# Up-projection units of a convolutional feed-forward: fewer pairs with a unit, another order inside

## The chip, the cores and the metric

The kernel runs on one core of one Trainium2 chip. The metric is the device time of one execution in microseconds, as the median of several runs; lower is better. Every input and weight is float32 and lies in the chip's memory.

## What is computed

A trunk of two layers over 256 positions of width 2048: mixer A (grouped-query attention), a feed-forward, mixer B (dilated windows), a second feed-forward, and a last normalisation. The change lies in the two feed-forwards:

```python
def conv_ffn(h, w_up, conv_w, conv_b, w_down):
    u = h @ w_up                       # 2048 -> 2 * 5632
    u = depthwise_conv(u, conv_w) + conv_b    # width 3 over positions
    gate, val = jnp.split(u, 2, axis=-1)
    return (jax.nn.silu(gate) * val) @ w_down

h = h + conv_ffn(rms_norm(h, ffn_norm[i]), w_up[i], conv_w[i], conv_b[i], w_down[i])
```

## The kernel before

**Products.** Every float32 weight tile of 128 x 1024 is loaded (`raw`), rounded by ScalarE into a high part (`wh`, L144 or L180), and VectorE subtracts that to get the low part (`wl`, L145 or L181). The activations have such pairs too. A product is three matmuls: high by high, high by low, low by high. There are four buffers each for `raw`, `wh` and `wl`, and within a feed-forward every third `raw` comes from a further pool.

**Pairs.** The up-projection has 22 blocks of 512 columns: 11 for the gate, 11 for the value. Block p of the gate and block p of the value make a pair; in the code the first pair is p = 0. The pairs 0 to 5 are the first half, 6 to 10 the second; behind each half its part of the down-projection runs. The depth 2048 is cut into four groups `kg` of 512. A plain `feed` does one group of one block: 48 matmuls for both blocks, 24 each, which need two splits per block.

**Units.** In `fast_unit` one group of both blocks is done with seven block products instead of eight: 42 matmuls. It splits seven weight tiles, of which four are sums of others, formed in place by VectorE ahead of their split (L179): the dictionary `sums` says which, and the loop takes the products in the order 1, 2, 3, 5, 7, 6, 4. Before the change each such sum is told to issue only after the previous split (`tc.issue_after`). The unit's products go into four more accumulators (`ps`), which the lines L695 to L704 of `up_pair` recombine. `UP` names the pairs with a unit; `UP_ORDER` puts it fourth in the pair, behind three plain feeds of the gate and ahead of three of the value. The down-projections and mixer B's output projection have units too, with spots of their own for the sums (`spot`); those always had a free order of sums.

**Work beside the matmuls.** What follows a block (evacuation with the scale, transposition into `u` with VectorE and 16 GpSimd copies, the convolution on ScalarE and VectorE, the silu, the product, splitting the result) is written as generators: `gate_gen`, `value_gen`, `flush`. `start` runs one to its first `yield` and puts it into the list `pending`, which is worked off first in, first out. `step()` moves the first of `pending` on by one `yield`; `step(True)` moves all in the list `beside`. A plain feed calls `step` once per 128 rows of depth, in turn for the one and for the other list; a unit calls it after each of its seven products. The order of calls, with a priority for splits that places them 60 instructions ahead, decides in which order each engine has its instructions; each engine works in that order. `sums` (started ahead of the first feed of the half) prepares the activation's own sums for the units, in slots with the numbers 20 or 16; `bias_lines` prepares mixer B's bias in three slots.

## Time and profile before

| | us |
|---|---|
| median of 3 runs | 2245.68 |
| fastest, slowest | 2245.32, 2246.84 |
| the profiled execution's own time | 2248.19 |
| its span, first to last instruction | 2246.4 |
| PE, DVE, ACT, POOL busy | 2220.4, 1902.1, 1350.8, 745.0 |

The span is what the traced instructions cover; the execution's own time also has what lies around them. PE is TensorE, PEld its weight loads, DVE VectorE, ACT ScalarE, POOL GpSimd, SP the engine that issues most loads. Busy time is the union of the shown durations; a matmul's shown duration overlaps the next one's, so a busy PE can still lose time between the starts of its matmuls. A row of a list of groups has line, engine, operation, output <- inputs, shapes and count, then busy time and mean duration in ns, then the idle time before and who ended it.

### The profile page before, as it was taken

What the parts mean: (1) busy time and instruction counts of PE and PEld (TensorE: products, weight loads), DVE (VectorE), ACT (ScalarE), POOL (GpSimd) and SP (SyncE); (2) the same over time, 40 slices, a digit from 0 to 9 for tenths busy, and PEclk for the clock granted to TensorE, in tenths of its full rate; (3) what the DMA queues carried; (4) which work ended last, traced back from release to release, by engine and by line L of the source; (5) the groups of instructions that cost most, each with busy time, mean ns of one, the idle gap of its engine ahead of it and who ended that gap; (6) DMA issues with size and microseconds to landing.
All of it is one profiled execution on the core that took longest, in us unless ns stands there. A gap on an engine that the chain in (4) does not pass through costs nothing.

```text
span 2246.4 us, 28935 instructions
## 1 busy us (share of the span) xinstructions
PE 2220.4 (99%) x9945; PEld 1830.8 (81%) x9945; DVE 1902.1 (85%) x2415; ACT 1350.8 (60%) x1902; POOL 745.0 (33%) x1017
## 2 busy tenths in 40 slices
PE   9999999999999999999999999999999999999998
PEld 7888888888887788888888888888887878877887
DVE  6877678998899997968886878687899998999887
ACT  7666656666455566665454456566666755556664
POOL 2333254652004662030053006003645600255511
PEclk9999999999999999999999999999999999999999
DMA  8665665565656566666656555656566565646664
GB/s 304 192 213 175 221 193 184 194 197 194 205 182 208 178 205 197 197 188 199 189 185 196 180 187 186 193 186 213 169 204 198 196 197 193 204 160 207 224 196 142
DMA packets 126181, 439.60 MB, mean 196 GB/s; under 512 B 14408, under 2 KB 18248, under 8 KB 126032
## 3 DMA queue, kind: packets, MB, share of 16 engines
q1 hardware_dynamic: 123056, 429.05, 58.7%
q0 software_dynamic: 2688, 8.39, 1.5%
q8 instruction: 78, 1.28, 0.2%
q14 instruction: 71, 0.58, 0.1%
q10 hardware_dynamic: 288, 0.30, 0.0%
HBM read 432.34 MB, written 5.34 MB: 195 GB/s over the span
## 4 chain that ended last, share of the span: by engine, by line
PE 43%; DVE 9%; issue 2%; DMA 1%; ACT 1%; POOL 1%; DVEq 0%; POOLq 0%; ACTq 0%
PE acc L133 13%; PE acc L132 13%; PE acc L134 13%; DVE wl L145 3%; DVE wl L181 2%; DVE raw L179 1%; DMA raw<-in_w_b_dram 1%; PE ps L188 1%; PE ps L189 1%; PE ps L187 1%; DVE cv L549 1%; DMA raw<-in_w_down_dram 0%; DVE tT L386 0%; PE acc L188 0%; PE acc L187 0%
## 5 line engine op out<-in xcount | busy, mean ns | idle before, releaser
L145 DVE TENSOR_TENSOR wl<-raw,wh 128x1024 fp32r<-128x1024 f32 (+1 forms) x708 | 882.6, 1258 | 199.6 <-ACT wh L144 194.5
L144 ACT ACTIVATE wh<-raw 128x1024 fp32r<-128x1024 f32 (+1 forms) x708 | 737.1, 1048 | 517.5 <-PE acc L134 404.1
L133 PE MATMUL acc<-wl,xh 128*128 128x512 f32 x2016 | 787.5, 391 | 2.7 <-DVE wl L145 2.5
L132 PE MATMUL acc<-wh,xh 128*128 128x512 f32 x2016 | 786.2, 391 | 0.0
L134 PE MATMUL acc<-wh,xh 128*128 128x512 f32 x2016 | 785.3, 390 | 0.0
L562 POOL COPY u<-quad 32x256 f32<-32x256 f32 x672 | 503.1, 749 | 463.3 <-DVE quad L377 426.2
L133 PEld LDWEIGHTS acc<-wl,xh 128*128 128x128 f32 x2016 | 379.1, 188 | 85.7 <-DVE wl L145 9.2
L134 PEld LDWEIGHTS acc<-wh,xh 128*128 128x128 f32 x2016 | 378.8, 188 | 78.7
L132 PEld LDWEIGHTS acc<-wh,xh 128*128 128x128 f32 x2016 | 379.2, 188 | 77.8
L132 PE MATMUL acc<-wh,a 128*128 128x512 f32 x720 | 280.9, 390 | 0.0
L133 PE MATMUL acc<-wl,a 128*128 128x512 f32 x720 | 280.4, 389 | 0.0
L134 PE MATMUL acc<-wh,a 128*128 128x512 f32 x720 | 280.0, 389 | 0.0
L180 ACT ACTIVATE wh<-raw 128x1024 fp32r<-128x1024 f32 x126 | 133.3, 1059 | 121.6 <-PE acc L134 72.2
L181 DVE TENSOR_TENSOR wl<-raw,wh 128x1024 fp32r<-128x1024 f32 x126 | 156.9, 1248 | 8.5 <-ACT wh L180 7.9
L134 PEld LDWEIGHTS acc<-wh,a 128*128 128x128 f32 x720 | 135.1, 188 | 28.3 <-DVE a L328 0.2
L133 PEld LDWEIGHTS acc<-wl,a 128*128 128x128 f32 x720 | 135.2, 188 | 28.0 <-DVE wl L145 0.5
L132 PEld LDWEIGHTS acc<-wh,a 128*128 128x128 f32 x720 | 135.2, 188 | 27.5
L381 POOL COPY wide<-quad 32x256 f32<-32x256 f32 x133 | 89.7, 674 | 168.2 <-DVE quad L377 159.8
L398 POOL COPY wide<-quad 32x256 f32<-32x256 f32 x88 | 53.1, 603 | 241.9 <-DVE quad L377 174.8
L489 ACT ACTIVATE stg<-acc,rstd 128x512 f32<-128x512 f32 x122 | 81.3, 681 | 28.8 <-PE acc L134 15.9
L549 DVE SCALAR_TENSOR_TENSOR cg<-u,cw,cg 128x256 f32<-128x256 f32 x176 | 92.7, 570 | 3.3 <-ACT cg L541 3.2
L549 DVE SCALAR_TENSOR_TENSOR cv<-u,cw,cv 128x256 f32<-128x256 f32 x176 | 90.0, 565 | 0.2
(309 smaller groups left out, 2267.6 us busy)
## 6 DMA issues: line engine op xcount, KB each, us to landing
raw<-in_w_up_dram SPq DMA_DIRECT2D x352, 512.0 KB, 4.5
raw<-in_w_down_dram SPq DMA_DIRECT2D x176, 512.0 KB, 4.6
raw<-in_w_b_dram SPq DMA_DIRECT2D x144, 512.0 KB, 4.4
raw<-in_w_bo_dram SPq DMA_DIRECT2D x48, 512.0 KB, 4.3
raw<-in_w_a_dram SPq DMA_DIRECT2D x40, 512.0 KB, 4.8
raw<-in_w_ao_dram SPq DMA_DIRECT2D x32, 512.0 KB, 4.6
raw<-in_w_a_dram SPq DMA_DIRECT2D x16, 256.0 KB, 6.0
there<-quad POOLq DMA_DIRECT2D x6, 512.0 KB, 3.8
```

Source lines behind the costliest of these rows:

```text
L132: nc.tensor.matmul(accs[m], xh, wh[:, j, :], start=st, stop=False)
L133: nc.tensor.matmul(accs[m], xh, wl[:, j, :], start=False, stop=False)
L134: nc.tensor.matmul(accs[m], xl, wh[:, j, :], start=False, stop=sp)
L144: nc.scalar.activation(wh[:, c], r[:, c], AF.Copy)
L145: newest[0] = nc.vector.tensor_tensor(wl[:, c], r[:, c], wh[:, c].bitcast(F32), ALU.subtract)
L180: nc.scalar.activation(wh, r, AF.Copy)
L181: done = nc.vector.tensor_tensor(wl, r, wh.bitcast(F32), ALU.subtract)
L381: nc.gpsimd.tensor_copy(o[32 * c:32 * c + 32, :, 32 * q:32 * q + 32], quad[32 * q:32 * q + 32, c])
L398: nc.gpsimd.tensor_copy(dst, src)
L489: nc.scalar.activation(o[:, m, :], accs[m], AF.Copy, scale=rstd[:, m:m + 1])
L549: nc.vector.scalar_tensor_tensor(cj, halves(flat[:, j, o:o + NT])[:, ::-1], tap(n, j, i), cj, ALU.mult, ALU.add)
L562: nc.gpsimd.tensor_copy(o, src)
```

## The change

`UP` loses the pair p = 7, so the third, fifth, seventh and ninth pair (p = 2, 4, 6, 8) have a unit, and the eighth is done with plain feeds. The sums of a unit are no longer told to follow the previous split. In an up-projection unit (`spot is None`) the loop no longer calls `step`. The gate's generator of a pair with a unit is put into `beside` instead of `pending`, and takes three more yields ahead of the last pair's product. The slots of `sums` are 16 in both halves, and `bias_lines` uses the slots 22, 20 and 14 for 14, 16 and 18.

```diff
-UP = 2, 4, 6, 7, 8
+UP = 2, 4, 6, 8
...
                 if q in sums:
-                    with tc.issue_after(done.ins) if spot is None else ExitStack():
-                        nc.vector.tensor_tensor(*sums[q], ALU.add)
+                    nc.vector.tensor_tensor(*sums[q], ALU.add)
                 nc.scalar.activation(wh, r, AF.Copy)
-                done = nc.vector.tensor_tensor(wl, r, wh.bitcast(F32), ALU.subtract)
+                nc.vector.tensor_tensor(wl, r, wh.bitcast(F32), ALU.subtract)
...
             begun.add(q)
-            step(i % 2 == 0)
+            if spot is not None:
+                step(i % 2 == 0)
...
                 if value is not None:
-                    for _ in range(2 if blk[0] == 1 else 1):
+                    for _ in range(4 if blk[0] in UP else 2 if blk[0] == 1 else 1):
                         yield
...
                     def gate_done(accs, gate=gate, last_value=last_value):
-                        start(gate_gen(accs, gate, last_value))
-
-                    first = partial(sums, 0, (20, 16)[hf], cg, cv)
+                        gen = gate_gen(accs, gate, last_value)
+                        if gate[0] in UP:
+                            next(gen)
+                            beside.append(gen)
+                        else:
+                            start(gen)
+
+                    first = partial(sums, 0, 16, cg, cv)
...
-        oc, oh, ln = (pair_slot(kt, [P, 1024], dt, t) for kt, t, dt in ((14, "oc", F32), (16, "oh", F32R), (18, "ln", F32)))
+        oc, oh, ln = (pair_slot(kt, [P, 1024], dt, t) for kt, t, dt in ((22, "oc", F32), (20, "oh", F32R), (14, "ln", F32)))
```

Around the unit a line of the change has a number lower by one: its sums are L178, its splits' two halves L179 and L180, its matmuls L186 to L188.

VectorE's order in the unit of the fifth pair in the first feed-forward, before. L181 is a split, L179 a sum of weights; L321 splits the activation of the third pair.

```order
L145 TENSOR_TENSOR wl_4286<-raw_4263,wh_4285 128x1024
L181 TENSOR_TENSOR wl_4315<-raw_4306,wh_4314 128x1024
L181 TENSOR_TENSOR wl_4325<-raw_4308,wh_4324 128x1024
L179 TENSOR_TENSOR raw_4306<-raw_4306,raw_4312 128x1024
L321 TENSOR_TENSOR s_4340<-st_4334,s_4339 128x1024
L181 TENSOR_TENSOR wl_4349<-raw_4310,wh_4348 128x1024
L179 TENSOR_TENSOR raw_4312<-raw_4312,raw_4310 128x1024
L181 TENSOR_TENSOR wl_4360<-raw_4306,wh_4359 128x1024
L179 TENSOR_TENSOR raw_4310<-raw_4306,raw_4310 128x1024
L181 TENSOR_TENSOR wl_4371<-raw_4312,wh_4370 128x1024
L179 TENSOR_TENSOR raw_4308<-raw_4310,raw_4308 128x1024
L181 TENSOR_TENSOR wl_4382<-raw_4310,wh_4381 128x1024
```

The same place in the change, where L180 is the split and L178 the sum:

```order
L145 TENSOR_TENSOR wl_4286<-raw_4263,wh_4285 128x1024
L180 TENSOR_TENSOR wl_4315<-raw_4306,wh_4314 128x1024
L178 TENSOR_TENSOR raw_4306<-raw_4306,raw_4312 128x1024
L178 TENSOR_TENSOR raw_4312<-raw_4312,raw_4310 128x1024
L180 TENSOR_TENSOR wl_4325<-raw_4308,wh_4324 128x1024
L180 TENSOR_TENSOR wl_4335<-raw_4310,wh_4334 128x1024
L178 TENSOR_TENSOR raw_4310<-raw_4306,raw_4310 128x1024
L178 TENSOR_TENSOR raw_4308<-raw_4310,raw_4308 128x1024
L180 TENSOR_TENSOR wl_4346<-raw_4306,wh_4345 128x1024
L180 TENSOR_TENSOR wl_4357<-raw_4312,wh_4356 128x1024
L180 TENSOR_TENSOR wl_4368<-raw_4310,wh_4367 128x1024
L180 TENSOR_TENSOR wl_4379<-raw_4308,wh_4378 128x1024
```

All four sums stand ahead of the fourth split, two of them ahead of the second, and the activation's split is no longer among them.

The activation's work of the third pair, which stood in that unit, stands in the change behind it, in the plain feeds of the value (L617 forms differences, L321 splits):

```order
L617 TENSOR_TENSOR st_4439<-cv_3358 128x256 x2
L617 TENSOR_TENSOR st_4439<-cv_3358,st_4439 128x256
L145 TENSOR_TENSOR wl_4639<-raw_4620,wh_4638 128x1024
L617 TENSOR_TENSOR st_4439<-cv_3358,st_4439 128x256
L377 STREAM_TRANSPOSE quad_4583<-stg_4551 128x16x32
L145 TENSOR_TENSOR wl_4659<-raw_4654,wh_4658 128x1024
L321 TENSOR_TENSOR s_4445<-st_4439,s_4444 128x1024
L321 TENSOR_TENSOR sx_4446<-cv_3358,sx_4446 128x512
L321 TENSOR_TENSOR sx_4446<-cv_3358,sx_4446 128x256
L377 STREAM_TRANSPOSE quad_4583<-stg_4551 128x16x32
L145 TENSOR_TENSOR wl_4677<-raw_4656,wh_4676 128x1024
```

The three L321, one of them in the middle of the unit before and two at its end, now come among the splits of plain feeds.

VectorE's order at the ninth pair's unit in the first feed-forward, before, where the pair ahead of it also had a unit (L549 is the convolution of the gate):

```order
L145 TENSOR_TENSOR wl_6831<-raw_6810,wh_6830 128x1024
L549 SCALAR_TENSOR_TENSOR cg_6322<-u_5954,cw_555,cg_6322 128x256 x4
L181 TENSOR_TENSOR wl_6865<-raw_6856,wh_6864 128x1024
L549 SCALAR_TENSOR_TENSOR cg_6322<-u_5954,cw_555,cg_6322 128x256 x3
L181 TENSOR_TENSOR wl_6875<-raw_6858,wh_6874 128x1024
L179 TENSOR_TENSOR raw_6856<-raw_6856,raw_6862 128x1024
L181 TENSOR_TENSOR wl_6889<-raw_6860,wh_6888 128x1024
```

And in the change:

```order
L145 TENSOR_TENSOR wl_6796<-raw_6791,wh_6795 128x1024
L549 SCALAR_TENSOR_TENSOR cg_6322<-u_5954,cw_555,cg_6322 128x256 x2
L145 TENSOR_TENSOR wl_6816<-raw_6793,wh_6815 128x1024
L180 TENSOR_TENSOR wl_6845<-raw_6836,wh_6844 128x1024
L178 TENSOR_TENSOR raw_6836<-raw_6836,raw_6842 128x1024
L178 TENSOR_TENSOR raw_6842<-raw_6842,raw_6840 128x1024
L180 TENSOR_TENSOR wl_6855<-raw_6838,wh_6854 128x1024
```

The convolution's last operations stand ahead of the plain feed's last split, none between the unit's own.

## The prediction

> **What bounds the kernel now.** I read the page's first part, then the list of what TensorE (PE) waits for, then the order of time on PE and VectorE (DVE) inside the units, then the busy time by stages. The page calls PE busy for 99% of the span, but that share hides the waits, as the next rows show. In the PE rows below the columns are start, duration, engine, line; the idle time before and what ended it stand in brackets. The first two rows frame a unit of the output projection without a wait, the others are the ninth pair's unit of the first feed-forward.
>
> ```profile
> PE 2220.4 (99%) x9945; PEld 1830.8 (81%) x9945; DVE 1902.1 (85%) x2415; ACT 1350.8 (60%) x1902; POOL 745.0 (33%) x1017
> ...
> 1481.31 0.39 PE L187 MATMUL ps<-wh,a 128*128 128x512 f32 x1
> ...
> 1490.60 0.39 PE L189 MATMUL acc<-wh,a 128*128 128x512 f32 x1
> ...
> 750.32 0.39 PE L187 MATMUL ps<-wh,xh 128*128 128x512 f32 x1
> ...
> 757.38 0.40 PE L187 MATMUL ps<-wh,s 128*128 128x512 f32 x1
> 758.79 0.50 PE L188 MATMUL ps<-wl,s 128*128 128x512 f32 x1 [1.02 <-DVE wl L181]
> 759.13 0.40 PE L189 MATMUL ps<-wh,s 128*128 128x512 f32 x1
> ...
> 763.69 0.39 PE L189 MATMUL acc<-wh,xh 128*128 128x512 f32 x1
> ```
>
> A unit has 42 matmuls, so 41 steps in 1490.60 - 1481.31 = 9.29 us: a matmul costs 0.2266 us, though it is shown as 0.39. A wait of 1.02 us therefore costs more than it says: 758.79 - 757.38 = 1.41, and 0.34 to the next, is 1.29 us over two clean steps, so about 0.275 us beyond the idle time shown. The ninth pair's unit takes 763.69 - 750.32 = 13.37 us; clean, with one foreign matmul in it, it would be 42 x 0.2266 = 9.52. It loses 3.85 us.
>
> The list of waits on PE (total, times, longest) says how much that is in all:
>
> ```profile
> PE ps L188 <- DVE wl L181: 9.6, 17, 1.0
> PE acc L133 <- DVE wl L145: 2.5, 7, 0.7
> ...
> PE acc L187 <- ACT wh L180: 1.3, 2, 0.6
> ```
>
> All 17 and both of the third row lie in the ten up-projection units (by windows: one wait in each third and seventh pair's unit, two in the fifth's, two and three in the eighth's, three in the ninth's). That is 10.9 us shown, plus 19 x 0.275 = 5.2, so 16.1. The ninth unit by this rule loses 2.7 + 0.8 = 3.5 of its 3.85; for short gaps under the listing I add 0.2 for each of the eighth and ninth units of both layers. **The up-projection units lose 16.9 us in all.**
>
> Why they lose it is in DVE's order of time. In the fifth pair's unit (PE enters it at 450.16):
>
> ```profile
> 450.16 0.39 PE L187 MATMUL ps<-wh,xh 128*128 128x512 f32 x1
> ...
> 437.24 14.40 POOL L562 COPY u<-quad 32x256 f32<-32x256 f32 x15
> ...
> 444.35 1.23 DVE L181 TENSOR_TENSOR wl<-raw,wh 128x1024 fp32r<-128x1024 f32 x1 [0.74 <-ACT wh L180]
> 446.06 1.30 DVE L181 TENSOR_TENSOR wl<-raw,wh 128x1024 fp32r<-128x1024 f32 x1 [0.49 <-ACT wh L180]
> 447.29 1.42 DVE L179 TENSOR_TENSOR raw<-raw,raw 128x1024 f32<-128x1024 f32 x1
> 448.63 1.42 DVE L321 TENSOR_TENSOR s<-st,s 128x1024 fp32r<-128x1024 f32 x1
> 449.97 1.42 DVE L181 TENSOR_TENSOR wl<-raw,wh 128x1024 fp32r<-128x1024 f32 x1
> 451.31 1.42 DVE L179 TENSOR_TENSOR raw<-raw,raw 128x1024 f32<-128x1024 f32 x1
> 452.64 1.21 DVE L181 TENSOR_TENSOR wl<-raw,wh 128x1024 fp32r<-128x1024 f32 x1
> 453.78 1.21 DVE L179 TENSOR_TENSOR raw<-raw,raw 128x1024 f32<-128x1024 f32 x1
> ```
>
> DVE is never idle from 447.29 on. One product's six matmuls take 1.36 us of PE; DVE owes it a split (L181) and for four of seven products a sum (L179), each 1.34 us from start to start beside the copies of GpSimd (POOL) and 1.13 without. Late in the unit every product costs DVE two operations, so PE waits. What saves a unit is the lead with which DVE enters it: sums need no free wl buffer, splits do.
>
> **The change, part by part.** (1) *Free order of sums, and no other work inside.* With the order that now stands in the fifth pair (split, sum, sum, split, split, sum, sum, four splits; L321 gone to the feeds behind), I walk on from the same first split. 444.35 + 1.13 = 445.5; two sums to 448.2; two splits to 450.9; two sums to 453.3 (the copies end at 437.24 + 14.40 = 451.6, 1.13 from there); the split of the fourth product ends at 454.4. PE asks for it after three products and one matmul: 450.16 + 19 x 0.2266 = 454.5. From there DVE needs 1.13 and PE 1.36 for each: no wait is left, with a margin of 0.1. The first sum also needs the unit's fourth weight load. Its issue and the time to landing:
>
> ```profile
> 432.31 6.31 SPq L167 DMA_DIRECT2D raw<-in_w_up_dram  x4
> ...
> raw<-in_w_up_dram SPq DMA_DIRECT2D x352, 512.0 KB, 4.5
> ```
>
> 432.31 + 6.31 + 4.5 = 443.1, ahead of the first split at 444.35, so the freed order does not run into it. The ninth pair now stands behind a plain pair with the same DVE rows as the fifth, so the same walk holds. Before, DVE came to it late:
>
> ```profile
> 746.36 1.41 DVE L181 TENSOR_TENSOR wl<-raw,wh 128x1024 fp32r<-128x1024 f32 x1
> ```
>
> that is 750.32 - 746.36 = 4.0 us ahead instead of 450.16 - 444.35 = 5.8. The third pair's unit has a lead of 361.90 - 355.36 = 6.5 and one short wait, which goes too:
>
> ```profile
> 355.36 1.31 DVE L181 TENSOR_TENSOR wl<-raw,wh 128x1024 fp32r<-128x1024 f32 x1 [0.93 <-ACT wh L180]
> ...
> 361.90 0.39 PE L187 MATMUL ps<-wh,xh 128*128 128x512 f32 x1
> ```
>
> I leave 0.1 us for each of these six units, 0.6.
>
> The seventh pair's unit keeps its wait. What stands between its splits was begun in the steps ahead of it, not inside it:
>
> ```profile
> 663.25 0.39 PE L187 MATMUL ps<-wh,xh 128*128 128x512 f32 x1
> ...
> 670.67 0.50 PE L188 MATMUL ps<-wl,s 128*128 128x512 f32 x1 [0.24 <-DVE wl L181]
> ...
> 657.42 1.24 DVE L181 TENSOR_TENSOR wl<-raw,wh 128x1024 fp32r<-128x1024 f32 x1
> 658.56 0.70 DVE L211 TENSOR_TENSOR h<-h,fold 128x512 f32<-128x512 f32 x1
> 659.16 1.24 DVE L321 TENSOR_TENSOR s<-cv,s 128x1024 fp32r<-128x1024 f32 x1
> ```
>
> L211 and L321 still stand among its splits, the same twelve operations end with the sixth product's split, so it is as late as before: 0.24 + 0.275 = 0.5, twice: 1.0. Of 16.9 us, 15.3 go.
>
> (2) *Eighth pair without a unit.* 48 matmuls for 42, in two layers: 12 x 0.2266 = 2.7 us more on PE, which nothing hides. Its waits were counted in (1). It also relieves DVE by three splits, four sums and eight operations of the recombination per layer:
>
> ```profile
> L181 DVE TENSOR_TENSOR wl<-raw,wh 128x1024 fp32r<-128x1024 f32 x21 | 27.1, 1290 | 0.7 <-ACT wh L180 0.7
> ...
> L179 DVE TENSOR_TENSOR raw<-raw,raw 128x1024 f32<-128x1024 f32 x12 | 15.7, 1306 | 0.0
> ...
> L698 DVE TENSOR_TENSOR acc<-acc,junk 128x512 f32<-128x512 f32 x3 | 2.1, 698 | 0.0
> ```
>
> 3 x 1.29 + 4 x 1.31 + 8 x 0.70 = 14.7 us. That is why the ninth pair regains its lead.
>
> (3) *The deferred work.* Splits of the activation (L607, L321) and steps of convolution go behind the unit into plain feeds; the gate's line runs beside them. Whether DVE has room there, the stages show (length, then busy time and instructions of PE, PEld, DVE, ACT, POOL): fourth, eighth, ninth and tenth pair of the first feed-forward.
>
> ```profile
> 388.30:431.80 43.50, 43.03 (x189) 34.66 (x188) 41.77 (x55) 25.40 (x33) 31.17 (x41) 1.00 0.52 174
> ...
> 689.70:733.90 44.20, 42.94 (x187) 34.58 (x186) 41.47 (x50) 27.08 (x33) 24.61 (x37) 1.00 0.57 189
> 733.90:779.90 46.00, 43.33 (x188) 34.59 (x187) 45.92 (x55) 28.17 (x37) 25.30 (x31) 1.00 0.55 182
> 779.90:823.40 43.50, 43.38 (x192) 35.59 (x191) 43.35 (x55) 26.57 (x35) 28.21 (x40) 1.00 0.55 176
> ```
>
> From the seventh pair on, 14.7 us fewer suffice. In the fourth pair DVE has only 43.50 - 41.77 = 1.7 us to spare, and some of PE's 2.5 us of waits at L133 lie there. What moves behind the third unit are four operations like this one:
>
> ```profile
> 760.93 0.41 DVE L607 TENSOR_TENSOR a<-cv,a 128x256 fp32r<-128x256 f32 x1
> ```
>
> 1.6 us against 1.7 free. So neither a new wait is sure there nor that the old ones go, and I take no change; the bounds are the old waits gone (about -1.5) and the waits of (1) back (the first rival).
>
> (4) *The slots.* The one-hot cast moves ahead of 24 copies on POOL, and may wait there for its slot's former tenant; the copies behind it come 17.58 us after the last:
>
> ```profile
> 212.96 4.34 POOL L398 COPY wide<-quad 32x256 f32<-32x256 f32 x8 [17.58 <-DVE quad L377]
> ```
>
> The cast and its wait fit into that; nothing on PE hangs on it. Uncovered it would cost the lateness itself, a few us once.
>
> The sum against the profiled span: 2246.4 - 15.3 + 2.7 = 2233.8; that execution's own time is 2248.19, 2.5 us above the median of the runs, 2245.68. From the median: 2245.68 - 12.6 = **2233.1 us**. What a measurement of this kernel can tell from no change is about 0.2%, 4.5 us, so from 2241.2 to 2250.2 is "same".
>
> **The rivals.** *The waits move into the feeds.* For it: DVE's 1.7 us in the fourth pair. Against it: the seventh to tenth pairs get 14.7 us of room. Price: the third and fifth units' waits of both layers come back at L133, two times 0.5 + 1.35, or 3.7: 2236.8 us.
>
> *Units that start late, slower.* The sums now stand ahead of the second to fourth split. If DVE enters a unit with the ninth's old lead of 4.0 us and all beside POOL copies, the fourth product's split, its eighth operation, ends 8 x 1.34 - 4.0 = 6.7 us into the unit, and PE wants it at 19 x 0.2266 = 4.3: 2.4 + 0.275 = 2.7 us in each of eight units, 21.6; 2245.7 + 2.7 - 16.9 + 21.6 = 2253 us. It decides from a lead of about 4.9 us downward (1.8 us per unit eat 16.9 - 2.7). Against it: three of the units before had 5.8 or more, and only the one right behind another unit had 4.0.
>
> *Nothing that can be told.* A lead between these, in half of the units, or the deferred work late for the down-projection: some 2243 us. Against the latter: DVE's order is the same again from the middle of the sixth pair to the seventh's unit and from the tenth pair on.
>
> *POOL's copies hold DVE up in full.* If a DVE operation with two SBUF inputs had to sit out a whole copy, 14.40 / 15 = 0.96 us each, not the 0.2 that the rows show (1.42 against 1.21), the eighth operation beside copies would end 8 x (1.13 + 0.96) - 5.8 = 10.9 us into the fifth's and ninth's units, 6.6 us late, over four units 26: 2259 us. The rows of the fifth unit, taken beside such copies, speak against it.
>
> The Trainium skill (SBUF — State Buffer, section Who interferes with whom) states this as a rule: a DVE instruction with two SBUF inputs contends with a GpSimd one that reads SBUF, and the loser fully blocks. By it the sum would be that rival's; the trace agrees that they contend, but shows 0.2 us, not a block.
>
> **How the numbers follow.** Forecast 0.70; waits moved into the feeds 0.18; late units 0.05; nothing to be told 0.05; full block 0.02. The likeliest gives 2233; its own range is 2230 (the L133 waits gone and the residues too) to 2236. The range reaches up through the first rival, with room for its waits to be half as large again and a unit or two short of lead: 2229.5 to 2240. Faster 0.88, same 0.05, slower 0.07.
>
> **What would show it.** Right: eight units of 42 matmuls, each about 9.3 to 9.6 us from first to last, but the seventh pair's near 10; the waits on the split of L180 (the line after the change) near 0.5 us in two or three places; the eighth pair without unit lines, DVE idle in it. The first rival: new rows L133 waiting on L145 some 20 to 60 us behind the third and fifth units. Late units: the fourth product's first wl matmul waiting in most units. Wrong altogether: PE waiting elsewhere, on accumulators or at the down-projection, in places without a wait before.

## The result, and the profile after

| | before | after |
|---|---|---|
| median, us | 2245.68 (2244.42 to 2248.61, 11 runs) | 2242.09 (2238.26 to 2244.5, 11 runs) |
| ratio, 95% interval | | 0.998 [0.9971, 0.9989] |
| the profiled execution: its time, its span | 2248.19, 2246.4 | 2243.49, 2241.7 |
| PE, DVE, ACT, POOL busy | 2220.4, 1902.1, 1350.8, 745.0 | 2219.9, 1879.4, 1344.0, 763.5 |

The change is faster by 0.2%: 3.6 us by the medians, where 12.6 were forecast and 2240 was the range's upper end. All that was forecast of the up-projection units came. Most of it was lost again in and just ahead of one unit, in a place that the prediction had ruled out.

The list of PE's waits after (total, times, longest). The unit's splits are L180 now, its matmuls L186 to L188:

```profile
PE acc L133 <- DVE wl L145: 5.1, 13, 0.7
PE acc L187 <- DVE wl L180: 4.5, 4, 1.9
...
PE ps L187 <- DVE wl L180: 0.4, 1, 0.4
```

The row of 9.6 us in 17 waits has shrunk to the last one here, in the seventh pair's unit. New is a row of four waits on `acc`, up to 1.9 us. The plain feeds' row, L133, has doubled from 2.5.

Where in the program that is shows in the busy time by stages (start and end; length; then busy time and instructions of PE, PEld, DVE, ACT, POOL; granted clock). The stages run from the third pair's unit to the second down-projection unit of the first half, and from there to the first unit of the second half's down-projection; first layer, then second. First the kernel before, then the changed one:

```profile
361.90:568.71 206.81, 205.35 (x900) 167.66 (x898) 193.50 (x238) 131.17 (x171) 93.20 (x121) 1.00 0.59 196
568.71:916.45 347.74, 343.19 (x1502) 280.63 (x1500) 315.03 (x371) 208.72 (x261) 117.53 (x163) 1.00 0.59 194
1626.07:1832.42 206.35, 204.94 (x895) 167.09 (x894) 193.01 (x235) 131.20 (x171) 92.05 (x120) 1.00 0.59 195
1832.42:2170.57 338.15, 332.50 (x1454) 271.52 (x1452) 308.07 (x360) 199.51 (x245) 120.21 (x161) 1.00 0.60 196
```

```profile
360.72:571.71 210.99, 207.15 (x900) 168.84 (x898) 195.18 (x239) 131.15 (x173) 103.17 (x123) 0.99 0.56 193
571.71:915.49 343.78, 342.72 (x1507) 282.02 (x1506) 301.34 (x355) 206.11 (x257) 118.30 (x163) 1.00 0.59 196
1625.53:1834.11 208.58, 205.80 (x895) 168.53 (x894) 193.81 (x237) 131.06 (x173) 93.48 (x122) 0.99 0.57 194
1834.11:2165.86 331.75, 331.50 (x1460) 273.36 (x1458) 294.08 (x344) 196.95 (x241) 120.15 (x161) 1.00 0.59 200
```

The second halves are shorter by 3.96 and 6.40 us, the first halves longer by 4.18 and 2.23. In the second halves DVE is rid of 13.7 and 14.0 us, near the 14.7 worked out. In the first halves its work is as much as before, and the granted clock is 0.99.

The loss sits in the first unit of the first half's down-projection. Its PE rows after (42 matmuls, clean 9.29 us):

```profile
546.84 0.39 PE L186 MATMUL ps<-wh,sx 128*128 128x512 f32 x1
...
548.96 0.50 PE L187 MATMUL acc<-wl,sx 128*128 128x512 f32 x1 [0.37 <-DVE wl L180]
...
552.49 0.50 PE L187 MATMUL acc<-wl,s 128*128 128x512 f32 x1 [1.88 <-DVE wl L180]
...
554.20 0.63 PE L186 MATMUL ps<-wh,s 128*128 128x512 f32 x1
554.62 0.63 PE L187 MATMUL ps<-wl,s 128*128 128x512 f32 x1
555.05 0.63 PE L188 MATMUL ps<-wh,s 128*128 128x512 f32 x1
...
560.60 0.39 PE L188 MATMUL acc<-wh,sx 128*128 128x512 f32 x1
```

560.60 - 546.84 = 13.76 us, 4.4 more than the 9.3 to 9.4 it takes clean. 2.8 of them are the two waits for splits and what they cost beyond the idle time shown; 1.6 are some eight matmuls behind the second wait that start 0.43 us apart instead of 0.2266 (the granted clock is 0.50 from 553.20 to 556.60). In the second layer the same unit takes 13.77.

DVE's rows around it say why. Before, with the time at which PE entered the unit (548.18) and reached the third product's second matmul:

```profile
538.50 1.22 DVE L578 TENSOR_TENSOR cv<-cg,cv 128x1024 f32<-128x1024 f32 x1
540.43 1.23 DVE L179 TENSOR_TENSOR u<-raw,raw 128x1024 f32<-128x1024 f32 x1 [0.72 <-DMA raw<-in_w_down_dram]
...
547.45 2.48 DVE L179 TENSOR_TENSOR u<-u,raw 128x1024 f32<-128x1024 f32 x2
549.85 1.22 DVE L181 TENSOR_TENSOR wl<-raw,wh 128x1024 fp32r<-128x1024 f32 x1
...
548.18 0.39 PE L187 MATMUL ps<-wh,sx 128*128 128x512 f32 x1
...
551.12 0.50 PE L188 MATMUL acc<-wl,s 128*128 128x512 f32 x1
```

The third split ended at 549.85 + 1.22 = 551.07; PE wanted it at 551.12. The margin was 0.05 us, as good as none. After:

```profile
539.36 1.22 DVE L578 TENSOR_TENSOR cv<-cg,cv 128x1024 f32<-128x1024 f32 x1
541.80 1.23 DVE L178 TENSOR_TENSOR u<-raw,raw 128x1024 f32<-128x1024 f32 x1 [1.22 <-DMA raw<-in_w_down_dram]
542.94 1.22 DVE L145 TENSOR_TENSOR wl<-raw,wh 128x1024 fp32r<-128x1024 f32 x1
...
548.83 2.48 DVE L178 TENSOR_TENSOR u<-u,raw 128x1024 f32<-128x1024 f32 x2
551.22 1.22 DVE L180 TENSOR_TENSOR wl<-raw,wh 128x1024 fp32r<-128x1024 f32 x1
...
544.22 0.50 PE L133 MATMUL acc<-wl,a 128*128 128x512 f32 x1 [0.59 <-DVE wl L145]
```

The same order, 1.37 us later, while PE came 1.34 earlier. I call **lead** the time from the start of DVE's first sum of this unit to PE's first matmul of it: 548.18 - 540.43 = 7.75 before, 546.84 - 541.80 = 5.04 after.

Two more things stand in these rows. The first sum waits for a weight load (0.72 us of idle before, 1.22 after): the operation ahead of it, L578, is only 0.86 us later than before, and the other 0.50 is the load. And behind the first sum stands the last split L145 of the plain feeds ahead of the unit, for which PE waits until 544.22.

### The profile page after: what moved, and what is told of

The parts are those of the page before. It is cut to its first block, busy times and chain, and to the rows that moved or that the text cites. A ratio compares the mean times of both kernels' runs of the same rounds, so it can differ in the third digit from the quotient of the medians.

```text
span 2241.7 us, 28897 instructions
## 1 busy us (share of the span) xinstructions
PE 2219.9 (99%) x9957; PEld 1835.3 (82%) x9957; DVE 1879.4 (84%) x2385; ACT 1344.0 (60%) x1894; POOL 763.5 (34%) x1017
## 4 chain that ended last, share of the span: by engine, by line
PE 43%; DVE 9%; issue 2%; POOL 1%; DMA 1%; ACT 1%; DVEq 0%; POOLq 0%; ACTq 0%
PE acc L133 13%; PE acc L134 12%; PE acc L132 12%; DVE wl L145 3%; DVE wl L180 1%; DVE cv L549 1%; PE ps L187 1%; PE ps L188 1%; PE ps L186 1%; POOL u L562 1%; PE acc L187 1%; PE acc L188 1%; DVE cg L549 1%; PE acc L186 1%; DMA raw<-in_w_b_dram 0%
## 5 line engine op out<-in xcount | busy, mean ns | idle before, releaser
L145 DVE TENSOR_TENSOR wl<-raw,wh 128x1024 fp32r<-128x1024 f32 (+1 forms) x716 | 899.1, 1264 | 226.9 <-ACT wh L144 221.1
L144 ACT ACTIVATE wh<-raw 128x1024 fp32r<-128x1024 f32 (+1 forms) x716 | 746.1, 1048 | 519.2 <-PE acc L134 407.0
L133 PE MATMUL acc<-wl,xh 128*128 128x512 f32 x2048 | 799.3, 390 | 4.2 <-DVE wl L145 4.1
L132 PE MATMUL acc<-wh,xh 128*128 128x512 f32 x2048 | 799.1, 390 | 0.3 <-ACT wh L144 0.3
L134 PE MATMUL acc<-wh,xh 128*128 128x512 f32 x2048 | 797.1, 389 | 0.0
L562 POOL COPY u<-quad 32x256 f32<-32x256 f32 x672 | 518.5, 772 | 444.2 <-DVE quad L377 394.9
L133 PEld LDWEIGHTS acc<-wl,xh 128*128 128x128 f32 x2048 | 384.7, 188 | 88.2 <-DVE wl L145 10.1
L132 PEld LDWEIGHTS acc<-wh,xh 128*128 128x128 f32 x2048 | 384.7, 188 | 79.9 <-ACT wh L144 0.7
L134 PEld LDWEIGHTS acc<-wh,xh 128*128 128x128 f32 x2048 | 384.6, 188 | 79.4
L133 PE MATMUL acc<-wl,a 128*128 128x512 f32 x720 | 280.7, 390 | 1.1 <-DVE wl L145 0.9
L179 ACT ACTIVATE wh<-raw 128x1024 fp32r<-128x1024 f32 x112 | 118.3, 1060 | 106.5 <-PE acc L134 76.4
L133 PEld LDWEIGHTS acc<-wl,a 128*128 128x128 f32 x720 | 135.2, 188 | 30.0 <-DVE wl L145 2.8
L180 DVE TENSOR_TENSOR wl<-raw,wh 128x1024 fp32r<-128x1024 f32 x112 | 135.6, 1228 | 5.8 <-ACT wh L179 4.4
L489 ACT ACTIVATE stg<-acc,rstd 128x512 f32<-128x512 f32 x122 | 81.2, 681 | 21.4 <-PE acc L134 13.3
L549 DVE SCALAR_TENSOR_TENSOR cg<-u,cw,cg 128x256 f32<-128x256 f32 x176 | 90.8, 560 | 1.9 <-ACT cg L541 1.9
L549 DVE SCALAR_TENSOR_TENSOR cv<-u,cw,cv 128x256 f32<-128x256 f32 x176 | 86.9, 540 | 0.0
```

The costliest lines, as they stand in the source:

```text
L132: nc.tensor.matmul(accs[m], xh, wh[:, j, :], start=st, stop=False)
L133: nc.tensor.matmul(accs[m], xh, wl[:, j, :], start=False, stop=False)
L134: nc.tensor.matmul(accs[m], xl, wh[:, j, :], start=False, stop=sp)
L144: nc.scalar.activation(wh[:, c], r[:, c], AF.Copy)
L145: newest[0] = nc.vector.tensor_tensor(wl[:, c], r[:, c], wh[:, c].bitcast(F32), ALU.subtract)
L179: nc.scalar.activation(wh, r, AF.Copy)
```

## The experiments

In the tables "lost" is the time by which matmuls of 512 columns start more than 0.2266 us apart, added up from the trace's PE rows over a unit or between units; two numbers are the two layers. "Down unit" is the first unit of the first half's down-projection. The ratio is to the kernel before, timed beside each on its own chip. There the kernel before took 2248.46 us beside the first four runs, 2249.68 beside the next four, 2249.72 beside the four behind those and 2248.58 beside the last two. So compare ratios, not times; the expectations' times are meant against 2245.68.

**Theory 1, the amount:** the first half has more work for DVE than time, so what PE loses there is conserved: freed in the units, it comes back at the down unit. **Theory 2, the deferred work:** the gate's line in the other list and the steps taken out of the units make DVE late there. **Theory 3** was formed after up_468: a chain from the sixth pair's gate to the down unit got longer. The first four expectations were written ahead of theory 1. They speak of a "theory of the lead" (DVE comes too late to that unit) in its place, and count the lead from the unit's first split (4.5 before, 1.75 in the change).

*One group of plain feeds more ahead of the down unit* (late_unit):

```diff
+if ns[0] == 0:
+    order = both[0] + both[3] + both[4] + f0 + [(5, 0)] + f1 + [(5, 1)]
```

> The changed kernel, but in the first half's first down-projection pair both feeds of the fifth group come ahead of the first unit (before: one of them ahead, one behind). Theory of the lead (VectorE enters that unit only 1.75 us ahead of TensorE, 4.5 before the change): one more feed is 24 x 0.2266 = 5.4 us of lead for the sums and splits, the unit takes about 9.3 us instead of 13.8 in both layers, without slow-clock matmuls, and the time falls by 8 to 9 us from the changed kernel, to some 2233 to 2235. Theory of the deferred work (the activation itself comes late because the gate's line and the steps were moved): the wait only moves to the next feed that needs the late data, and the time stays within 2 us of the changed kernel, 2240 to 2244.

2239.59 us, ratio 0.9959 [0.9945, 0.9973]. The down unit loses 1.55 and 1.55, all matmuls at full pace. That is nearer to the theory of the lead, but short of it: the unit takes 10.91 us, not 9.3, and 0.9959 of 2245.68 is 2236.5, not 2233 to 2235.

*Half of the 16 copies of the sixth pair's gate on ScalarE* (gate_by_act):

```diff
-turned(s, blk[1])
+turned(s, blk[1], blk[0] == HALVES[0][1] - 1)
```

> The changed kernel, but of the sixth pair's gate half of the 16 transposing copies go to ScalarE, as the sixth pair's value already does. Theory of the lead, with GpSimd's copies (14.9 us, ending 517.85) as the late link ahead of the convolution: the convolution of that gate starts some 5 us earlier, VectorE's queue ahead of the first down-projection unit ends earlier, the unit's lead comes back to 4 us or more, and the time falls to 2234 to 2237. If VectorE's own queue is the link, not the copies: the convolution starts earlier but the first split of the unit moves by less than 1 us, and the time stays at 2240 to 2244.

2239.76 us, 0.9961 [0.9946, 0.9976]. Lead 5.58 and 5.72, the down unit loses 3.86 (with slow matmuls) and 2.12 (without). So shorter copies there do bring DVE earlier, but by little: counted from the first split the lead is 2.3 and 2.4, where 4 or more was expected. The time, 0.9961 of 2245.68 or 2236.9, lies at the upper edge of 2234 to 2237.

*The kernel before with the smaller `UP` alone* (only_up; `UP = 2, 4, 6, 8`):

> The kernel before with the eighth pair's unit alone taken out, everything else as before. Theory of the lead: the second halves gain as in the changed kernel (eighth unit's waits 2.1 and 2.5 us gone, the ninth's 3.75 reduced to the fifth's 1.4 at most, 2.7 us of matmuls added in all), the first halves keep their waits in the third and fifth units and have no new one in the down-projection: 2237 to 2240, so faster than the changed kernel. If the eighth pair's removal is what hurts: 2243 or more.

2241.41 us, 0.9968 [0.9957, 0.998]. The units keep their waits (0.43 to 1.52 lost in each), the down unit loses 0.46 and 0.41. That is as expected, and this one line brings at least as much as the whole change.

*The change with steps and the gate's line as before, free sums and `UP` kept* (steps_back):

```diff
-            if spot is not None:
-                step(i % 2 == 0)
+            step(i % 2 == 0)
...
+                        start(gate_gen(accs, gate, last_value))
```

> The changed kernel with the steps inside the units and the gate's line in the common list again, so of the change only the pairs, the free sums and the slots. Theory of the lead: the units of the third and fifth pair keep small waits (under 0.6 us each), TensorE is early at the down-projection all the same, and the wait there stays at 2 us or more: 2239 to 2243. Theory of the deferred work: the first down-projection unit has no wait over 0.6 us, as before the change: 2234 to 2237.

2245.22 us, 0.9986 [0.9977, 0.9995]. Lead 7.96 and 7.42; the down unit loses 0 and 0.44, but the third and fifth pairs' units 0.45 to 1.14 each, and the feeds ahead of the fifth 2.19 and 1.56. So the down unit has no wait over 0.6, as theory 2 said, but the time that theory 2 said (2234 to 2237) did not come. Beside only_up, on the same chip, the free sums gain nothing. From the third pair's unit to the end of the first half the lost time is 4.1 to 5.0 us in seven of the eight layers of these four runs (3.2 in late_unit's second; 1.6 of the 5.0 in gate_by_act's first are slow matmuls), and in the change 5.5 and 4.1 without the slow matmuls. That looked like theory 1.

*The third pair plain too* (up_468; `UP = 4, 6, 8`), which takes 14.7 us from DVE in each first half:

> The change, but the third pair is also done with plain feeds, so the first half of each feed-forward has one unit (the fifth pair's) instead of two. PE gets 6 more matmuls in each layer, 2 x 6 x 0.2266 = 2.7 us; DVE is rid of three splits, four sums and eight operations of the recombination, 14.7 us in each first half by the rows of before, and of four operations on the activation. Theory 1 (the first half has more DVE work than time, so the loss is conserved and shows at the first down-projection unit): the loss there goes (4.4 in each layer to under 1), the first half as a whole loses 2 to 3 us instead of 7.1 and 5.7, so the time is 2 x 4 - 2.7, some 5 us below the change: ratio to the kernel before about 0.9955. Theory 2 (the order of the deferred work, with the gate's line in the other list, makes the down-projection late; the amount is beside the point): the fifth pair's deferred work stays where it is, the unit there still loses about 4 us, and the time is the change's + 2.7: ratio about 0.999.

2245.34 us, 0.9981 [0.9972, 0.999]. Its down unit:

```profile
542.54 1.23 DVE L178 TENSOR_TENSOR u<-raw,raw 128x1024 f32<-128x1024 f32 x1 [0.88 <-DMA raw<-in_w_down_dram]
...
553.23 0.50 PE L187 MATMUL acc<-wl,s 128*128 128x512 f32 x1 [1.87 <-DVE wl L180]
```

PE enters at 547.59: lead 5.05, 4.38 lost, as in the change. 14.7 us less work, in the third pair, whose unit stood 186 us ahead, move nothing. **Theory 1 falls** as it was put (it had 0.9955, theory 2 had 0.999): lost time is not conserved over the half.

*The eighth pair's unit back, all else as in the change* (up_five; `UP = 2, 4, 6, 7, 8`):

> The change with the eighth pair's unit back (third, fifth, seventh, eighth, ninth), all else as in the change. PE does 12 matmuls less (2.7 us), DVE has 14.7 us more in each second half. Theory 1 (DVE's amount decides): the second half is again short of DVE time, and the losses of before return there, about 5 us in each layer, in the eighth's and ninth's units or, since the units' own order is freed, behind them in feeds or at the down-projection; ratio to the kernel before 0.9995 to 1.001. Theory 2 (the order decides): the freed order keeps the eighth's and ninth's units free of waits as it does the third's and fifth's, and the kernel gains the 2.7 us: ratio about 0.997.

2251.86 us, 1.0008 [0.9999, 1.0017]. The list of waits:

```profile
PE ps L187 <- DVE wl L180: 6.4, 6, 2.2
```

The eighth and ninth units lose 1.12 and 5.01 us, in the second layer 1.06 and 3.40: together 6.1 and 4.5, against 5.9 and 6.2 before. That is what theory 1 had forecast here, and theory 2's 0.997 did not come. For two units in a row the free sums and the steps moved out bring little; that the ninth is clean in the change comes from the eighth's being gone (in only_up, with the old order, the ninth loses 0.51).

*Idle operations of VectorE, 8 in each layer* (dose_first in the third to sixth pairs, dose_second in the seventh to tenth; one at each gate as below, one more at each value):

```diff
+if gate[0] in (2, 3, 4, 5):
+    nc.vector.tensor_reduce(dose, nhalf[:, :, None].to_broadcast([P, 8, 160]), axis=AX.X, op=ALU.max)
```

> The change with two idle operations of VectorE more in each of the third to sixth pairs (a maximum over 1280 columns of a constant into a small tile of its own, nobody reads it; by 1.25 us for 1024 columns about 1.5 us each), 8 in each layer, about 12 us of DVE in each first half. Theory 1 (DVE has no time to spare in the first half): most of it is paid, 8 to 12 us in each layer, so 16 to 24 us over the change, and the lost time of PE shows again at the third and fifth units, in the feeds and at the first down-projection unit. Theory 2 (DVE has room and only the order at the first down-projection unit is bad): under 6 us in all.

0.9993 [0.9984, 1.0002], and 0.9989 [0.998, 0.9998] for the other, of which theory 1 had expected 0 to 5 us over the change and theory 2 as much as of the first. Both missed their places: the operations depend on nothing, they all started in the first 81 us of the program, and DVE's busy time in the stages is within 1.6 us of the change's. They say nothing on the theories.

*Steps inside the unit of the fifth pair only* (steps_in_fifth):

```diff
-            if spot is not None:
+            if spot is not None or inside[0]:
...
+                        inside[0] = p == 4
```

> The change, but the fifth pair's unit calls the steps after its products as before; every other unit does not. Theory 3: from the sixth pair's gate (its copy out of the accumulators by ScalarE) a chain runs over VectorE's transposes, the 16 GpSimd copies and the convolution to VectorE's first sum of the first down-projection unit. The work put off from the fifth unit stands ahead of and inside this chain and lengthens it, from 39.7 us before to 41.7, so that VectorE enters that unit with 5.04 us of lead in every kernel of this order (whatever else is added or taken away), not 7.4 to 8. Here the order in the sixth pair is that of before again, so the lead is again 7.4 or more, the down unit loses under 0.5 instead of 4.4 in each layer, the fifth pair's unit again 1.1 to 1.4: 2 x 3 us less than the change, ratio to the kernel before about 0.9955. Theory 1 (lost time is conserved over the first half): as much comes back elsewhere, and the ratio stays at 0.998.

2238.12 us, 0.9945 [0.9932, 0.9957]. I follow the chain from where ScalarE copies the sixth pair's gate out of the accumulators (L489). Before, as rows of ScalarE, DVE and POOL, with the silu of the fifth pair's gate (L588) in front:

```profile
494.67 1.06 ACT L588 ACTIVATE cg<-cg 128x1024 f32<-128x1024 f32 x1 [2.35 <-DVE cg L549]
...
500.72 1.24 ACT L489 ACTIVATE stg<-acc,rstd 128x512 f32<-128x512 f32 x2
...
501.47 1.29 DVE L377 STREAM_TRANSPOSE quad<-stg 128x512 f32<-128x512 f32 x2
...
502.90 14.08 POOL L562 COPY u<-quad 32x256 f32<-32x256 f32 x16 [3.54 <-DVE quad L377]
```

In steps_in_fifth:

```profile
499.69 1.29 DVE L377 STREAM_TRANSPOSE quad<-stg 128x512 f32<-128x512 f32 x2
...
501.12 14.08 POOL L562 COPY u<-quad 32x256 f32<-32x256 f32 x16 [3.88 <-DVE quad L377]
...
539.20 1.23 DVE L178 TENSOR_TENSOR u<-raw,raw 128x1024 f32<-128x1024 f32 x1 [0.91 <-DMA raw<-in_w_down_dram]
```

and in the change, with the splits L607 that now stand ahead of the transposes and the convolution on ScalarE that waits for the copies:

```profile
499.17 1.06 ACT L588 ACTIVATE cg<-cg 128x1024 f32<-128x1024 f32 x1 [2.34 <-DVE cg L549]
500.14 1.25 ACT L489 ACTIVATE stg<-acc,rstd 128x512 f32<-128x512 f32 x2
...
500.19 1.42 DVE L607 TENSOR_TENSOR a<-cv,a 128x256 fp32r<-128x256 f32 x4
501.54 1.29 DVE L377 STREAM_TRANSPOSE quad<-stg 128x512 f32<-128x512 f32 x2
...
502.96 14.89 POOL L562 COPY u<-quad 32x256 f32<-32x256 f32 x16 [6.87 <-DVE quad L377]
...
517.88 1.10 ACT L541 ACTIVATE cg<-u,cw 128x256 f32<-128x256 f32 x2 [3.76 <-POOL u L562]
```

In the change the gate leaves the accumulators at 500.14 and the first sum starts at 541.80: 41.7 us. Before (500.72 to 540.43) it was 39.7. The transposes start 1.40 us behind the copy-out instead of 0.75, the copies take 14.89 instead of 14.08, and the stretch from the copies' end to the sum is 0.5 longer, which is the wait for the load.

These 1.95 us are half of it. The copy-out itself comes late: 41.91 us behind the last matmul of the fifth pair's unit instead of 39.36. Two matmuls that now stand behind that unit are 0.45 of this; the other 2.1 are ScalarE, which does the silu of the fifth pair's gate just ahead of the copy-out and waits there for the convolution L549, part of the work put off from the fifth unit (499.17, before 494.67). 1.95 + 2.1 = 4.05, of which PE's own waits in the feeds ahead of the down unit (1.26) take 1.26 off: 2.8, against 2.71 of lead lost.

With the steps back in this one unit the order is the old one, the copies take 14.08, the lead is 7.65 and 7.55 and the down unit loses 0.21 and 0.31; the fifth pair's unit loses 1.13 and 1.09 again. Here the copy-out is again 39.37 behind the fifth unit. So moving the fifth unit's steps out of it frees that unit of 1.1 us and costs 4 in the next (1.6 of them slow matmuls), and about 1 in the feeds between.

*Sums of the first down-projection pair tied to the split before them* (tie_down):

```diff
+                    with tc.issue_after(newest[0].ins) if tied[0] else ExitStack():
+                        nc.vector.tensor_tensor(*sums[q], ALU.add)
```

> The change, with the first pair of down-projection blocks in each first half having its sums tied to the split before them again (the up-projection's stay free). The third product of a unit needs no sum, but with free sums its split stands behind three of them. Theory 3: the chain ahead stays as long as in the change, but the third split comes one sum (1.13 us) earlier and the unit's first two splits need no longer stand behind a sum that waits for the fourth load; what is left is 7 operations of 1.13 us against four products of 1.36, some 0.7 us late at the end. The unit loses 0.7 to 1.5 instead of 4.4, without the stretch of slow matmuls: 6 us less in both layers, ratio about 0.9955. Rival: VectorE's amount of work decides, and the wait only moves to the last products and into the feeds behind: ratio 0.997 to 0.998.

2239.1 us, 0.9949 [0.9935, 0.9962]. The down unit loses 1.58 and 1.57, in two waits at its end, as worked out from the number of operations (0.7) and a little more:

```profile
552.28 0.50 PE L188 MATMUL ps<-wl,s 128*128 128x512 f32 x1 [0.42 <-DVE wl L181]
554.55 0.50 PE L188 MATMUL ps<-wl,s 128*128 128x512 f32 x1 [0.61 <-DVE wl L181]
```

Here the old, tied order is the better one: the third product needs no sum, and with free sums its split stood behind all four.

*The sixth pair's gate transposed one yield earlier* (early_turn):

```diff
-                yield
+                if blk[0] != HALVES[0][1] - 1:
+                    yield
                 turned(s, blk[1])
```

> The change, but the sixth pair's gate is transposed right after it is copied out (its generator has one yield less), so that on VectorE two of the four splits L607 that stood ahead of the two transposes now stand behind the first of them or both. A small dose of theory 3: the chain begins 0.67 us earlier, so the lead at the down unit is 5.4 to 5.7 instead of 5.04, its third split 0.4 to 0.7 us earlier; the unit loses 3.7 to 4 or, if the wait gets short enough for the clock, 2.2: 1 to 4 us less than the change in both layers, ratio 0.9965 to 0.9976. Rival (the lead is set by loads and buffers near the unit, not by the chain): the lead stays 5.04 and the ratio 0.998.

2242.11 us, 0.9958 [0.9946, 0.9971]. Lead 5.44 and 5.81; the down unit loses 4.00 (with slow matmuls) and 2.05 (without). The lead moved, so the loads near the unit don't set it alone: in all thirteen kernels named under "Lead and loss" below DVE waits 0.4 to 1.3 us for that load, in those with a lead of 7.4 and more too. From the copy-out to the sum gate_by_act and early_turn take 39.6 to 40.0 us, as in the kernel before; but the copy-out stays 41.9 to 42.0 behind the fifth unit, and so the lead stays below 5.9. Of the changed kernels only those with the fifth unit's steps inside it (steps_in_fifth, steps_back) have the copy-out at 39.4 to 39.6 and a lead of 7.4 or more.

*late_unit and gate_by_act together* (late_and_act):

> Both single remedies measured so far together on the change: one group of plain feeds more ahead of the first down-projection unit, and half of the copies of the sixth pair's gate on ScalarE. Theory 3: the chain is 3 us shorter (copies of 6.6 instead of 15 us, but ScalarE does the other half in order) and the unit is 10.9 us of feeds further away, so the first down unit loses under 0.5 and nothing else appears: some 3 us below either alone, ratio 0.9945 to 0.995. Rival (conserved loss): as each alone, 0.996.

2235.4 us, 0.9932 [0.992, 0.9944]: the lowest ratio of all, below both kernels and below what was expected; its interval overlaps that of steps_in_fifth. (One group of feeds is 24 matmuls, 5.4 us, not the expectation's 10.9.) The down unit loses 0.29 and 0.37, and the waits on L187 for `acc` are gone from the list:

```profile
PE acc L133 <- DVE wl L145: 3.0, 7, 0.7
...
PE ps L187 <- DVE wl L180: 1.5, 4, 0.7
```

*2.96 us of idle DVE work that can't move ahead, at the sixth or at the fourth pair's gate* (dose_sixth, dose_fourth):

```diff
+                for _ in range(2 if blk[0] == 5 else 0):
+                    nc.vector.tensor_reduce(dose, s[:, 0, :8, None].to_broadcast([P, 8, 160]), axis=AX.X, op=ALU.max)
                 turned(s, blk[1])
```

> The change with two idle operations of VectorE more in each layer (a maximum over 1280 columns, 1.48 us each, 2.96 us in all, that reads the sixth pair's gate once it is copied out, so it can't move ahead of that; nobody reads its result). They stand inside the chain, between the copy out of the accumulators and the transposes. Theory 3 (that chain sets VectorE's lead at the first down-projection unit): the lead falls from 5.04 to 2 or less, and the unit loses 7 to 9 us instead of 4.4, in each layer; 5 to 9 us over the change in all, ratio to the kernel before about 1.001 (1.000 to 1.002). Theory 1 (the amount of VectorE's work in the first half decides, wherever it stands): the same time as with the same two operations in the fourth pair.

> The same two operations in each layer, placed in the same way at the fourth pair's gate, some 85 us earlier. Theory 3: VectorE has made up for them long before the sixth pair's gate; the lead at the first down-projection unit is 5.04 and the loss there 4.4 as in the change, and PE loses at most 1 to 2 us in each layer at the fifth pair's unit or in feeds ahead of it; ratio to the kernel before about 0.9985 (0.9975 to 0.9995). Theory 1: the same time as with the operations in the sixth pair, and the same loss at the down-projection.

| | ratio | lost at the fifth pair's unit | in the feeds ahead of the down unit | in the down unit | lead |
|---|---|---|---|---|---|
| the change | 0.998 [0.9971, 0.9989] | 0, 0 | 1.26, 0.88 | 4.40, 4.39 | 5.04, 5.04 |
| dose_sixth | 1.0004 [0.9995, 1.0013] | 0, 0 | 4.01, 4.21 | 2.79, 2.79 | 5.05, 5.04 |
| dose_fourth | 1.0011 [1.0001, 1.0021] | 5.30, 5.25 | 0.83, 0.52 | 2.80, 2.79 | 5.04, 5.05 |

Both expectations failed in part. The lead did not fall below 5.04: PE then waits in the last plain feed for the split right behind the unit's first sum (542.94 + 1.22 = 544.16 in the change, PE's matmul at 544.22), and from there the matmuls left are the same. The change itself stands at this floor already. What comes on top is paid in the feeds: 2.8 and 3.3 us more for 2.96 us of work. In time theory 1's forecast held: the two doses cost the same within the intervals, and the down unit loses 2.79 or 2.80 with either. And the fourth pair's dose was not made up for; PE paid for it at the next unit, 3.7 us and 1.6 in slow matmuls:

```profile
452.29 0.50 PE L188 MATMUL acc<-wl,xh 128*128 128x512 f32 x1 [1.02 <-DVE wl L181]
...
457.44 0.50 PE L188 MATMUL ps<-wl,s 128*128 128x512 f32 x1 [2.14 <-DVE wl L181]
```

Once paid there, it changed nothing at the down unit but the slow matmuls. So it seems that DVE has nothing to spare from the fourth pair to the down unit, and work put in is paid at the next place where DVE has to be ahead; but it is settled there, not carried on. That fits up_468 too: its work was taken out ahead of the fifth pair's unit, which lost nothing any more, and nothing was gained. It is an argument from these runs; no run tests it by itself.

**Lead and loss.** In all kernels with the same order of DVE at the down unit, lead and loss add up to one number:

| kernel | lead | lost in the down unit | of it in slow matmuls | lead + rest |
|---|---|---|---|---|
| before | 7.75, 7.56 | 0.11, 0.30 | 0 | 7.86, 7.86 |
| steps_in_fifth | 7.65, 7.55 | 0.21, 0.31 | 0 | 7.86, 7.86 |
| only_up | 7.39, 7.45 | 0.46, 0.41 | 0 | 7.85, 7.86 |
| gate_by_act | 5.58, 5.72 | 3.86, 2.12 | 1.6, 0 | 7.84, 7.84 |
| early_turn | 5.44, 5.81 | 4.00, 2.05 | 1.6, 0 | 7.84, 7.86 |
| the change | 5.04, 5.04 | 4.40, 4.39 | 1.6, 1.6 | 7.84, 7.83 |

steps_back has 7.96 and 0, 7.42 and 0.44; up_five, dose_second, dose_sixth and dose_fourth read 5.04 to 5.06 and 2.77 to 2.80, all without slow matmuls; up_468 and dose_first read as the change. Below 7.85 each us of lead lost is a us of PE.

## Why the prediction was wrong

*The waits of the up-projection units* (16.9 us, 15.3 to go): right. By the starts of matmuls the ten units lost 16.9 before, and the eight lose 1.2 now, all in the seventh pairs' units (10.30 and 10.02 us long, "near 10"); the other six take 9.29. So 15.7 went.

*The eighth pair plain, +2.7*: right. The second halves' stages gained 3.96 and 6.40, together 10.4. The working gives 9.2: the loss of their six units, 13.1 before (0.51, 2.09, 3.76, 0.52, 2.49, 3.75) less 1.2 that is left, less 2.7. These stages also begin with the second down-projection unit of the first half, which loses 0.54 and 1.22 less. That the ninth pair regains its lead by the eighth's relief, and not by the free order, is what up_five and only_up show.

*The deferred work, "I take no change"*: this is the step that failed. The bounds taken, -1.5 to +3.7, came from the room in the fourth pair's stage and looked only at the feeds behind the units. Those feeds did not change much: between the third and the fifth pair's unit they lose 1.41 and 0.46 us now, 1.06 and 1.09 before. It was in the rivals that the down-projection was dismissed: "DVE's order is the same again from the middle of the sixth pair". The order is, and the time is not. An equal order says what comes after what; whether PE waits depends on DVE's lead, and that at this unit was 7.75 with 7.85 needed, which stood in the rows of before (551.07 against 551.12). What PE gained in the third and fifth units without DVE's gaining it too could not be kept there; and DVE, with the fifth unit's steps behind it, was 1.37 us later. The sign that the prediction had named for being wrong altogether, PE waiting at the down-projection in places without a wait before, is the one that came. Measured: +4.29 and +4.09 in the down unit, +1.26 and +0.88 in the feeds ahead of it, 10.5 us in all; 0.54 and 1.22 less in the second down unit. That is 8.8 us net. The waits came out 0.4 better than the term, the feeds behind the third units 0.3; what is left, 8.1, is about the 7.9 by which the profiled execution missed (2241.7 against 2233.8; the medians missed by 9.0). 3.2 of the 8.8 are slow matmuls, which no term had, and which are luck: the traced execution is the only one in which they can be seen. If every run had them, the time without them would be some 2239 us, an estimate: inside the stated range, and the step would have failed all the same.

*The rivals*: "waits move into the feeds" (2236.8) was nearest in kind, but looked 20 to 60 us behind the units. "Nothing that can be told" (2243) named the deferred work late for the down-projection, and its time was right within 1 us, with the slow matmuls' help; it had 0.05. "Units that start late" did not come: all six others keep their lead. The copies did not hold DVE up in full (1.41 us instead of 1.21).

*The slots*: no row of PE's waits hangs on them.

## What to carry to other kernels

When a change frees an engine that was waiting, look for the next place where its supplier must be ahead, and read the margin there from the rows (the supply's end against the moment it is wanted), even where the order of work is untouched. Work moved out of one burst is paid at the next one unless there is idle time between: look for that idle time on the supplier first, and follow the late chain back through every queue: here half of the delay sat in ScalarE's, in front of the first row that looked late. A free order of preparation is good where each product needs one and bad where a product that needs none stands behind them all.

## What the runs showed of the hardware

Behind a wait of 1.88 us the next matmuls start 0.427 us apart (554.20 to 554.62 above) instead of 0.2266, eight of them, for 3.4 us, which costs 1.6 us more than the wait itself. It does not follow every such wait: in the change, up_468 and dose_first it came in both layers, in up_five, dose_second and dose_sixth, with the same 1.9 us waits in the same place, in none. By the traces' records of the granted clock each such stretch lasts 3.413 us, and within one trace they begin a whole number of 3.413 us apart (553.22 and 1816.15 in the change: 370 of them). On this grid the change's wait lies whole in the stretch ahead of the drop, 549.81 to 553.22; in up_five, whose grid is fixed by a drop at 757.78, the same wait is cut, with 1.54 us in the one stretch. All drops inside units came behind a stretch with 1.87 us or more of idle PE; two stretches with as much (one in gate_by_act, one in dose_fourth) had none behind them, so this is not the whole rule. The Trainium skill (TensorE: Matmul & The Clock Gate, Part 1: The HAM clock gate) gives 426.7 ns between the starts of 512-column matmuls at the half clock, and windows of about 3.4 us that run freely and are not tied to the kernel; pace and length agree with the rows. It asks for about one idle window of that length ahead of the drop; here 1.87 of the 3.41 us were enough at times.

The 16 copies of GpSimd took 14.08 us before and 14.89 in the change, where DVE was busy through all of them; the DVE operations beside them took 1.41 instead of 1.21. The Trainium skill (SBUF — State Buffer, Who interferes with whom) calls that contention an exclusive lock; the rows show 0.2 us for each operation, and 0.8 us for the sixteen copies.
